# Sums of the mixing layer's end on GpSimd and VectorE, and two pairs' weight sums moved into the attention: a decoder trunk on one Trainium2 core

## The chip, the core and the metric

One core of a Trainium2 chip (trn2) runs the whole kernel in one launch. The metric is the device time of one execution in microseconds, median of several runs; the profile is of one execution, with its own time beside it. Engines are named as in the profile: PE is TensorE, DVE is VectorE, ACT is ScalarE, POOL is GpSimd, SP is the engine that issues most DMAs.

## The reference

One decoder layer on 1024 tokens of width 1024, in float32:

```python
xn = rmsnorm(x, norm_mix_w)
da_q, da_k, da_v, sw_q, sw_k, sw_v, g_da, g_sw = split_cols(xn @ w_in)
y_da = diff_attention(da_q, da_k, da_v, lam, lam_init, subln_w)      # 4 heads, causal, ALiBi
y_sw = sliding_window_attention(sw_q, sw_k, sw_v, sinks)             # 8 heads, window 128
merged = sigmoid(g_da) * (y_da @ w_br_da) + sigmoid(g_sw) * (y_sw @ w_br_sw)
x = x + merged @ w_mix_out                                           # the mixing layer's end
xn = rmsnorm(x, norm_ffn_w)
x = x + conv_ffn(xn, w_up, conv_w, conv_b, w_down)                   # up-projection to 2 x 2816, conv, SwiGLU, down
return rmsnorm(x, norm_final_w)
```

## The kernel before, in words

Everything is held transposed: 128 channels on the partitions, tokens along the free dimension. Each float32 operand is split into a high part (cast on ScalarE) and a low part (the rest, subtracted on VectorE), and a product takes three matmuls of 128x128 by 128x512: high by high, high by low, low by high.

The large products use a two-by-two block scheme with seven products (P1 to P7, as in Strassen's and Winograd's forms) in place of eight. It needs sums of blocks: of the weights (S1 to S4) and of the activations (T1 to T4).

The stages, in order: `project` (input projection; nine pairs of column blocks through the seven products), `attention` (four differential heads u = 0 to 3, then two groups of sliding-window heads; gate projections are put between the blocks of queries), `rest` (branch products and gates), `mix` (merged @ w_mix_out), `hidden` (22 pairs of up-projection columns, each with convolution and SwiGLU), `down`.

**Weight sums.** The sums of the mixing layer's weights (`sums_of`, line 93) and of the first two up-projection pairs (`sums_up`, line 105; buffers `ud0`, `ud1` in DRAM) are made by DMA: a copy issued by SP, then adding DMAs issued by GpSimd. `sums_of` has 32 steps for the mixing weights and `sums_up` 16, eight copies and eight adds, each of 256 KB. Before, both are chained (line 486) and six steps are taken in each of the nine pairs of the projection (line 489), each queued behind the pair's last loads on SP (`self.sync`) and last sum on GpSimd (`self.sum`) by `issue_after`, which only fixes the order on an engine. The later pairs' sums are made on GpSimd in `sum_pair` (lines 143 to 146).

**The mixing layer's end** (`mix`, line 891). Fourteen half-stages i = 0 to 13, two for each of P1, P2, P5, P6, P3, P7, P4. Each has 24 matmuls (line 1034) and two evictions on VectorE (line 1037) that add a PSUM bank to `xm`, which holds the residual stream x. P1, P6, P7 and P4 share one set of four PSUM banks, so P4's second half may start only when P7's second half has been evicted. A finished half-row goes through `finish` (line 932): stored to DRAM, squared on ScalarE, and the squares added up on GpSimd (line 942) for the next RMSNorm.

While the last half-stages run, the activations for the first up-projection pair are made from `xm`. A hand-written table `due` (line 970) says after which half-stage which of them is traced; `run_due` queues them behind the last weight split. For each k = 0 to 3, with column block k and token halves 0 and 1:

- `scale2`: half 1 of row k is scaled by minus the norm weight, and added to half 0, which gives T1.
- `scale4`: half 1 of row k+4 is scaled into c22, which gives B22.
- `sums4`: c22 is added to half 1 of row k (which gives T3) and to half 0 of row k (which gives T2).
- `b21`, `scale3`: half 0 of row k+4 gives B21; scaled by minus the weight it is added to half 0 of row k, which gives T4.
- `t1` to `t4`, and the B forms, through `put` and `parts` (lines 914 to 928): cast on ScalarE, low part on VectorE.

Each of these sixteen sums is, before, an adding DMA from SBUF to SBUF, issued by GpSimd (`add`, line 930), so that the cast after it waits for a DMA to land.

The first pair's weights come in four parts (`part_pair`, line 117): part 0 is A11, A12; part 1 is S1, S2; part 2 is S3, S4; part 3 is A22. Each is a load by SP into one of three `raw` tiles, a cast on ScalarE (line 126) and a low part on VectorE (line 128). Before, part 1 is traced at half-stage 12 after the due work, part 0 at 13 ahead of the due work, part 2 at 13 after it, part 3 at the end. The first pair's products in `hidden` (line 1081) run in the order P1, P5, P3, P7, P2, then sixteen column sums of the squares (line 207), then P6, P4, then P1 and P2 of the second pair, and the spread of the reciprocal norms (line 222).

In `attention`, `da_at` (line 662) clears two blocks of the transposed weights on GpSimd (line 670) before each second block of queries, and `da_av` (line 708) multiplies them with the values after it, four times in a head. `v32` (line 643) loads a head's values through SP.

Of the kernel before, what the change touches and what calls it, by code (L numbers as in the profile page):

```python
# [3 lines left out]

# [1 line left out]

# [5 lines left out]
F32 = mybir.dt.float32  # L12
F32R = mybir.dt.float32r
AF = mybir.ActivationFunctionType
ALU = mybir.AluOpType
# [31 lines left out]
class Trunk:  # L47
# [260 lines left out]
    def project(self):  # L308
# [6 lines left out]
        with ExitStack() as ctx:  # L315
# [158 lines left out]
            for m in self.plain[3:]:  # L474
# [4 lines left out]
                if m == self.plain[3]:  # L479
                    with tc.issue_after(self.pow.ins), tc.high_priority(40):  # L480
                        wg, pg = self.next_w(), [bank() for _ in range(2)]
                    for hf in range(2):
                        self.mm3(pg[hf], wg, self.xact, hf)
            prods = (("P1", "A11", "B11"), ("P2", "A12", "B21"), ("P5", "S1", "T1"), ("P7", "S3", "T3"), ("P3", "S4", "B22"),
                     ("P6", "S2", "T2"), ("P4", "A22", "T4"))
            sums = chain(self.sums_of(self.md, self.w_mix, H2), self.sums_up())
            for j, ms in enumerate(self.pairs):
                w = self.next_w()
                for _ in range(6):
                    with tc.issue_after(self.sync), tc.issue_after(self.sum):  # L490
                        next(sums, None)
                pp = {}
                for name, a, b in (prods[i] for i in ((0, 1, 4, 2, 3, 5, 6) if j == 0 else (0, 1, 2, 5, 3, 4, 6))):
                    pp[name] = bank()
                    self.product(pp[name], w[a], b)
                us = [self.tl(tp, [P, T], "us", bufs=3) for _ in range(2)]
                self.recombine(pp, us, tp, 0)
                for m, u in zip(ms, us):
                    if self.kind[m] == "g":
                        nc.sync.dma_start(self.gd[m - 18], u)  # L500
                    else:
                        nc.gpsimd.tensor_tensor(u, u, self.rstd, ALU.mult)  # L502
                        self.keep(m, u, (tp, "hi"))
# [38 lines left out]
    def attention(self):  # L542
        nc, tc = self.nc, self.tc
        with ExitStack() as ctx:
            e = ctx.enter_context
            self.ap = e(tc.tile_pool(name="ap", bufs=1, side="right", reuse_waits="tile"))
            self.fpool = e(tc.tile_pool(name="fyp", bufs=1, side="right", reuse_waits="tile"))
            ap = self.ap

            lt = self.tl(self.gpool, [P, 64], "g", bufs=2)  # L550
            ls = self.st.tile([P, 4], F32, name="ls")
            for c in range(2):
                a = C_LAM + 128 * c
                nc.vector.tensor_tensor(lt, self.vecs[:, a:a + 64], self.vecs[:, a + 64:a + 128], ALU.mult)
                nc.vector.tensor_reduce(ls[:, c:c + 1], lt, axis=mybir.AxisListType.X, op=ALU.add)
            nc.scalar.activation(ls[:, 2:4], ls[:, 0:2], AF.Exp)
            self.neglam = self.cp.tile([P, 1], F32, name="neglam")
            nc.vector.tensor_tensor(self.neglam, ls[:, 3:4], ls[:, 2:3], ALU.subtract)
            nc.vector.tensor_scalar(self.neglam, self.neglam, LAM_INIT, None, ALU.subtract)
            self.nsink = self.cp.tile([P, 8], F32, name="nsink")  # L560
            nc.vector.tensor_scalar(self.nsink, self.vecs[:, C_SINK:C_SINK + 8], -1.0, None, ALU.mult)
            self.subw = self.cp.tile([P, 1], F32, name="subw")
            nc.vector.tensor_scalar(self.subw, self.vecs[:, C_SUB:C_SUB + 1], 1.0 - LAM_INIT, None, ALU.mult)

            self.bias = ap.tile([P, T + 256], F32, name="bias")
            nc.sync.dma_start(self.bias, self.bias_d)

            later = []
            st = self.q_stacks(0), self.kv_stacks(0)
            for b in self.back[0][0]:  # L570
                self.back_half(*b)
            for u in range(6):
                if st is None:
                    st = self.q_stacks(u), self.kv_stacks(u)
                if u < 4:
                    self.v_parts(u)
                elif u == 4:
                    self.sw_v(self.v32(17))
                y = self.tl(self.fpool, [P, T], "y", bufs=2) if u < 4 else None
                aT = None  # L580
                for i in range(NB):
                    if u < 4:
                        if i == 0:
                            self.s0 = self.tl(self.st, [P, NB], "s0", bufs=2)
                        if i % 2 == 0:
                            aT = self.da_at(i // 2)
                        self.da_step(u, i, st, aT)
                        if i % 2 == 1:
                            self.da_av(u, i // 2, aT, y)
                    else:  # L590
                        self.sw_step(u - 4, i, st)
                    for b in self.back[u + 1][i]:
                        self.back_half(*b)
                    self.flush(1)
                    if later:
                        later.pop(0)()
                st = None
                if u < 4:
                    later = self.da_norm(u, y)
            self.flush(0)  # L600
# [42 lines left out]

    def v32(self, m):
        v = self.tl(self.fpool, [P, T], "f", bufs=2)
        self.nc.sync.dma_start(v, self.qd[m, 0])
        return v

    def v_parts(self, u):
# [12 lines left out]
    def da_at(self, r):  # L662

        t = {}
        for g in range((2 * r + 2 + 3) // 4):
            for part in range(2):
                t[g, part] = self.tl(self.ap, [P, 4, 256], "aT", F32R, bufs=5)
        for part in range(2):
            j = 2 * r + 1
            self.nc.gpsimd.memset(t[j // 4, part][:, j % 4, 0:P].bitcast(F32), 0.0)  # L670
        return t

    def da_step(self, h, i, st, aT):
# [217 lines left out]
    def mix(self, M, mr, mctx):  # L891
# [35 lines left out]
            t = self.slot(k) if name == "T3" else self.slot(4 + k) if name == "B21" else up[name, k]  # L927
            self.B[name, k] = parts(t, src, scale)

        add = lambda x, y: nc.gpsimd.dma_start(x, y, accum_op=ALU.add)  # L930

        def finish(m, hf):
            x, k = col(m, hf), m % 4
# [15 lines left out]
        def scale2(k):  # L949
            x = col(k, 1)  # L950
            nc.scalar.mul(x, x, nw[:, k:k + 1])
            add(col(k, 0), x)

        c22 = lambda k: x22[k // 2][:, k % 2]

# [1 line left out]
            nc.scalar.mul(c22(k), col(k + 4, 1), wcol(k + 4))  # L957
            put("B22", k, c22(k))

        def sums4(k):  # L960
            add(col(k, 1), c22(k))
            add(col(k, 0), c22(k))

        def scale3(k):
            nc.scalar.mul(col(k + 4, 1), col(k + 4, 0), nw[:, k + 4:k + 5])
# [1 line left out]

        t1, t2, t3, t4 = (lambda k, n=n, h=h: put(n, k, col(k, h)) for n, h in (("T1", 0), ("T2", 0), ("T3", 1), ("T4", 0)))
        b21 = lambda k: put("B21", k, col(k + 4, 0), nw[:, k + 4:k + 5])
        due = {6: ((scale1, 0, 1),), 7: ((scale1, 2, 3),), 10: ((scale2, 0, 1),), 11: ((t1, 0, 1), (scale2, 2, 3), (scale4, 0, 1), (sums4, 0, 1)),  # L970
               12: ((scale4, 2, 3), (t1, 2, 3), (sums4, 2, 3), (t3, 0, 1)), 13: ((t3, 2, 3), (t2, 0, 1), (b21, 0), (scale3, 0), (b21, 1), (scale3, 1)),
               14: ((b21, 2), (t2, 2), (b21, 3), (t2, 3), (scale3, 2, 3), (t4, 0, 1), (t4, 2, 3))}

        def split_m(name, o, hf, scale=None):
            for k in range(4):
# [11 lines left out]
        with tc.tile_pool(name="psM", bufs=8, space=PSUM, reuse_waits="tile") as psM:  # L987
            chains = [[self.tl(psM, [P, H2], "m") for _ in range(4)] for _ in range(2)]
            for n, stage in enumerate(STAGES):
# [8 lines left out]
                for h in range(2):  # L998
                    with tc.high_priority(60):
                        w = self.next_w()  # L1000
                    if i == 13:
                        w0.update(self.part_pair(pair, 0))
                    if n == 0:
                        for m in (2 * h, 2 * h + 1, 2 * h + 4, 2 * h + 5):
                            nc.sync.dma_start(xm[m], self.xT[m])
                    run_due(i)
                    held = lows[-1] if lows else None
                    first = self.lo
                    if stage == "P4":
                        self.uw = uw  # L1010
                        w0.update(self.part_pair(pair, 1 + h))
                        self.uw = None
                    if h == 0:
                        with tc.issue_after(self.hi.ins), tc.issue_after(self.lo.ins):
# [453 lines left out]
```

## Time and profile before

| | us |
|---|---|
| median of 3 runs | 1337.36 (1334.35 to 1337.37) |
| profiled execution | 1337.29 |
| its span, first to last instruction | 1335.5 |
| TensorE busy | 1307.9 |
| VectorE busy | 1059.9 |
| ScalarE busy | 637.6 |
| GpSimd busy | 513.5 |

Places in the span, from the timeline: the projection ends near 238 us, the differential heads run to about 405, P7's second half of `mix` begins near 652, P4's second half at 665.65, the first up-projection pair at 678.49, and the long run of the other pairs goes from 718 to 1112. The matmuls' ends are modelled, and the spans of GpSimd are rough; a wait is put down to the instruction that released it last.

### The profile page before, as it was taken

To read this page: it belongs to the slowest core of one execution; us is meant where nothing else is said; L and a number is where in the kernel's file an instruction comes from. 1 tells how busy PE (TensorE), PEld (TensorE's weight loads), DVE (VectorE), ACT (ScalarE), POOL (GpSimd) and SP (SyncE) were. 2 spreads that over 40 slices of the span, in tenths; PEclk is the share of its full clock that TensorE was granted. 3 is DMA by queue.
4 is the path that set the end of the run, shared out by engine and by line. 5 is a ranking of instruction groups with operands and counts; after the bars stand their busy time and mean duration, and the time that the engine had idled before them with its cause. 6 is when DMAs were issued, how large, how long until landed. Compare 5 with 4: busy or idle time off the path is not lost.

```text
span 1335.5 us, 17341 instructions
## 1 busy us (share of the span) xinstructions
PE 1307.9 (98%) x6162; PEld 1086.4 (81%) x6162; DVE 1059.9 (79%) x1504; ACT 637.6 (48%) x1010; POOL 513.5 (38%) x411
## 2 busy tenths in 40 slices
PE   9999999999999999999979999999999999999997
PEld 7888888788888878888757888888888888888886
DVE  8845763389888977567567999999999999896865
ACT  8523231276667764335564343434344435554543
POOL 0456664000011015743444667676666742000002
PEclk9999999999999999999989999999999999999998
DMA  8356876976544236568693534663536227953534
GB/s 299 120 158 207 258 186 182 312 193 176 153 126 127 95 123 220 153 210 246 180 234 111 188 124 125 161 225 104 184 122 181 75 87 255 322 186 116 166 97 146
DMA packets 86598, 231.67 MB, mean 173 GB/s; under 512 B 9584, under 2 KB 17392, under 8 KB 86256
## 3 DMA queue, kind: packets, MB, share of 16 engines
q1 hardware_dynamic: 63264, 187.04, 41.6%
q0 software_dynamic: 10368, 26.22, 11.7%
q10 hardware_dynamic: 12880, 17.31, 3.6%
q8 instruction: 48, 0.79, 0.2%
q14 instruction: 38, 0.31, 0.1%
HBM read 173.39 MB, written 84.41 MB: 193 GB/s over the span
## 4 chain that ended last, share of the span: by engine, by line
PE 83%; POOL 4%; DMA 4%; issue 3%; DVE 2%; ACT 2%; SPq 0%; POOLq 0%; ACTq 0%; DVEq 0%
PE t L1061 34%; PE y L1281 9%; PE d L1281 7%; PE g L199 4%; PE g L200 4%; PE g L201 4%; PE m L1034 4%; PE sc L687 3%; POOL us L502 2%; PE t L703 1%; PE sc L201 1%; PE sc L200 1%; PE sc L199 1%; PE t L806 1%; PE sc L775 1%
## 5 line engine op out<-in xcount | busy, mean ns | idle before, releaser
L180 DVE TENSOR_TENSOR wl<-raw,wh 128x1024 fp32r<-128x1024 f32 (+2 forms) x91 | 107.8, 1186 | 48.9 <-ACT wh L178 40.9
L178 ACT CAST wh<-raw 128x1024 fp32r<-128x1024 f32 (+2 forms) x91 | 80.6, 887 | 105.0 <-PE y L1281 49.0
L1211 POOL TENSOR_TENSOR us<-us,rstd 128x1024 f32<-128x1024 f32 x42 | 95.4, 2319 | 48.3 <-DVE us L520 29.1
L1061 PE MATMUL t<-T,sh 128*128 128x512 f32 x352 | 108.5, 390 | 0.0
L216 POOL TENSOR_TENSOR rs<-ms,mhalf 128x8 f32<-128x8 f32 (+2 forms) x9 | 14.2, 1578 | 236.6 <-DVE ms L214 230.4
L143 POOL TENSOR_TENSOR sf<-rv 128x512 f32<-128x512 f32 x29 | 60.0, 2070 | 105.9 <-DMA rv<-in_w_up 48.0
L1225 ACT ACTIVATE c<-us,vecs 128x1024 f32<-128x1024 f32 x44 | 54.7, 1247 | 78.3 <-POOL us L1211 73.9
L157 ACT CAST sh<-sf 128x1024 fp32r<-128x1024 f32 x58 | 60.0, 1043 | 49.3 <-POOL us L1210 24.4
L159 DVE TENSOR_TENSOR sl<-sf,sh 128x1024 fp32r<-128x1024 f32 x58 | 74.2, 1280 | 10.7 <-ACT sh L157 10.7
L1061 PE MATMUL t<-x,wh 128*128 128x512 f32 x248 | 82.2, 389 | 0.0
L1061 PEld LDWEIGHTS t<-T,sh 128*128 128x128 f32 x352 | 65.9, 188 | 13.6
L199 PE MATMUL g<-xh,wh 128*128 128x512 f32 x176 | 71.1, 404 | 3.2 <-DVE u L518 1.8
L1228 DVE SCALAR_TENSOR_TENSOR c<-us,vecs,c 128x1024 f32<-128x1024 f32 x44 | 71.2, 1651 | 0.1
L1227 DVE SCALAR_TENSOR_TENSOR c<-us,vecs,c 128x1024 f32<-128x1024 f32 x44 | 68.5, 1585 | 2.6 <-ACT c L1225 2.6
L200 PE MATMUL g<-x,wh 128*128 128x512 f32 x176 | 70.5, 400 | 0.0
L201 PE MATMUL g<-xh,wl 128*128 128x512 f32 x176 | 70.3, 399 | 0.0
L1061 PE MATMUL t<-T,sl 128*128 128x512 f32 x176 | 68.5, 389 | 0.0
L1061 PE MATMUL t<-x,sh 128*128 128x512 f32 x212 | 68.2, 389 | 0.0
L1281 PE MATMUL y<-h,wh 128*128 128x512 f32 (+1 forms) x224 | 65.3, 375 | 0.0
L145 POOL TENSOR_TENSOR sf<-raw,rv 128x512 f32<-128x512 f32 x29 | 52.2, 1801 | 30.8 <-DVE sl L159 30.8
L159 DVE TENSOR_TENSOR wl<-raw,wh 128x1024 fp32r<-128x1024 f32 x29 | 63.8, 2199 | 0.1
L1034 PE MATMUL m<-x,wh 128*128 128x512 f32 x192 | 60.3, 396 | 2.4 <-DVE xm L1037 2.4
(340 smaller groups left out, 3954.4 us busy)
## 6 DMA issues: line engine op xcount, KB each, us to landing
u<-qd SPq DMA_DIRECT2D x72, 256.0 KB, 6.4
raw<-in_w_in SPq DMA_DIRECT2D x22, 512.0 KB, 5.5
raw<-in_w_up SPq DMA_DIRECT2D x22, 512.0 KB, 5.0
hd<-c SPq DMA_DIRECT2D x22, 512.0 KB, 2.6
sdP<-in_w_down POOLq DMA_DIRECT2D x16, 704.0 KB, 8.7
rv<-in_w_up SPq DMA_DIRECT2D x20, 512.0 KB, 4.5
hc<-hd SPq DMA_DIRECT2D x33, 256.0 KB, 4.6
gr<-gd SPq DMA_DIRECT2D x16, 512.0 KB, 4.6
```

What stands on the lines that cost most here:

```text
L159: low = nc.vector.tensor_tensor(lo, src, hi.bitcast(F32), ALU.subtract)
L178: self.hi = nc.scalar.copy(wh, raw)
L180: self.lo = (eng or nc.vector).tensor_tensor(wl, raw, wh.bitcast(F32), ALU.subtract)
L199: nc.tensor.matmul(ps, wh[:, kc + o, :], ah, start=first and n == 0, stop=False)
L200: nc.tensor.matmul(ps, wh[:, kc + o, :], al, start=False, stop=False)
L201: nc.tensor.matmul(ps, wl[:, kc + o, :], ah, start=False, stop=last and n == len(kcs) - 1)
L1034: nc.tensor.matmul(ps, v[:, m % 2 * 4 + k, :], x, start=start and k == j == 0, stop=k == 3 and j == 2, skip_group_check=True)
L1061: nc.tensor.matmul(ps, (ah, ah, al)[p][:, k, :], (bh, bl, bh)[p], start=first and n == p == 0, stop=last and p == 2 and n == len(ks) - 1, ...
L1211: i = (nc.vector if m % NF == 0 else nc.gpsimd).tensor_tensor(us[:, 2:], us[:, 2:], self.rstd, ALU.mult)
L1227: nc.vector.scalar_tensor_tensor(c, us[:, 1:T + 1], cw[1], c, ALU.mult, ALU.add)
L1228: nc.vector.scalar_tensor_tensor(c, us[:, 0:T], cw[0], c, ALU.mult, ALU.add)
L1281: nc.tensor.matmul(ps, v[:, k - k0, :], x, start=start and k == i == 0, stop=k == HK - 1 and i == 2, skip_group_check=True)
```

## The change

`add` becomes a `tensor_tensor` add in place, on GpSimd by default. The four adds of `scale2` and the first two of the new `sum3` go to VectorE, the other ten (`sum3` for k = 2, 3, four of `sum2`, four of `scale3`) to GpSimd. `sums4` is taken apart into `sum3` and `sum2`, and the order within `due` changes. Part 1 of the first pair's weights stays at half-stage 12, parts 0 and 2 are both traced at 13 ahead of the due work.

`sums_up` is no longer chained into the projection, which takes four steps a pair instead of six. One step of it is taken after each `da_av` of the four differential heads, queued on SP behind the head's load of v and on GpSimd behind the last clearing of blocks.

```diff
-            sums = chain(self.sums_of(self.md, self.w_mix, H2), self.sums_up())
+            sums = self.sums_of(self.md, self.w_mix, H2)
...
-                for _ in range(6):
+                for _ in range(4):
...
-            later = []
+            later, sums = [], self.sums_up()
...
                             self.da_av(u, i // 2, aT, y)
+                            with tc.issue_after(self.sync), tc.issue_after(self.sum):
+                                next(sums, None)
...
-        self.nc.sync.dma_start(v, self.qd[m, 0])
+        self.sync = self.nc.sync.dma_start(v, self.qd[m, 0]).ins
...
-            self.nc.gpsimd.memset(t[j // 4, part][:, j % 4, 0:P].bitcast(F32), 0.0)
+            self.sum = self.nc.gpsimd.memset(t[j // 4, part][:, j % 4, 0:P].bitcast(F32), 0.0).ins
...
-        add = lambda x, y: nc.gpsimd.dma_start(x, y, accum_op=ALU.add)
+        add = lambda x, y, eng=nc.gpsimd: eng.tensor_tensor(x, x, y, ALU.add)
...
-            add(col(k, 0), x)
+            add(col(k, 0), x, nc.vector)
...
-        def sums4(k):
-            add(col(k, 1), c22(k))
-            add(col(k, 0), c22(k))
+        sum3 = lambda k: add(col(k, 1), c22(k), nc.vector if k < 2 else nc.gpsimd)
+        sum2 = lambda k: add(col(k, 0), c22(k))
...
-        due = {6: ((scale1, 0, 1),), 7: ((scale1, 2, 3),), 10: ((scale2, 0, 1),), 11: ((t1, 0, 1), (scale2, 2, 3), (scale4, 0, 1), (sums4, 0, 1)),
-               12: ((scale4, 2, 3), (t1, 2, 3), (sums4, 2, 3), (t3, 0, 1)), 13: ((t3, 2, 3), (t2, 0, 1), (b21, 0), (scale3, 0), (b21, 1), (scale3, 1)),
-               14: ((b21, 2), (t2, 2), (b21, 3), (t2, 3), (scale3, 2, 3), (t4, 0, 1), (t4, 2, 3))}
+        due = {6: ((scale1, 0, 1),), 7: ((scale1, 2, 3),), 10: ((scale2, 0, 1),), 11: ((t1, 0, 1), (scale2, 2, 3), (scale4, 0, 1), (sum3, 0, 1), (sum2, 0, 1)),
+               12: ((t1, 2, 3), (t3, 0, 1), (scale4, 2, 3), (sum3, 2, 3), (sum2, 2, 3)), 13: ((t3, 2, 3), (t2, 0, 1), (b21, 0), (scale3, 0), (b21, 1), (scale3, 1)),
+               14: ((t2, 2, 3), (b21, 2), (scale3, 2), (b21, 3), (scale3, 3), (t4, 0, 1, 2, 3))}
...
                     if i == 13:
-                        w0.update(self.part_pair(pair, 0))
+                        self.uw = uw
+                        for part in (0, 2):
+                            w0.update(self.part_pair(pair, part))
+                        self.uw = None
...
-                    if stage == "P4":
+                    if i == 12:
                         self.uw = uw
-                        w0.update(self.part_pair(pair, 1 + h))
+                        w0.update(self.part_pair(pair, 1))
                         self.uw = None
```

1 line of the change is left out of this document (removed).

## The prediction, made before the result was known

> **What bounds the kernel now.** I read the page's busy line first, then TensorE's waits for the stretch in which the change works, then the engines' timelines there.
>
> ```profile
> PE 1307.9 (98%) x6162; PEld 1086.4 (81%) x6162; DVE 1059.9 (79%) x1504; ACT 637.6 (48%) x1010; POOL 513.5 (38%) x411
> ```
>
> TensorE is busy for 98% of the span. Its matmul count does not change, so time can only come from the places where it stands still or runs at a lower clock. Its waits from 640 to 720 us:
>
> ```profile
> PE t L1061 <- ACT wh L126: 7.0, 2, 5.5
> PE m L1034 <- DVE xm L1037: 2.4, 1, 2.4
> PE t L1061 <- ACT sh L126: 1.4, 1, 1.4
> PE t L1061 <- DVE wl L128: 1.4, 1, 1.4
> PE t L1061 <- DVE sl L128: 0.8, 1, 0.8
> ```
>
> These sum to 13.0 us. Where they lie, from TensorE's timeline (start, duration; the wait before it in brackets), then the chain's row for the long stretch behind them, then the windows' row for the stretch (length; busy TensorE, weight load, VectorE, ScalarE, GpSimd; granted clock, DMA share, GB/s):
>
> ```profile
> 662.90 0.39 PE L1034 MATMUL m<-x,wl 128*128 128x512 f32 x1
> 665.65 0.78 PE L1034 MATMUL m<-x,wh 128*128 128x512 f32 x2 [2.36 <-DVE xm L1037]
> ...
> 678.49 1.22 PE L1061 MATMUL t<-B,wh 128*128 128x512 f32 x2 [5.53 <-ACT wh L126]
> ...
> 688.04 0.73 PE L1061 MATMUL t<-B,sh 128*128 128x512 f32 x2 [1.43 <-ACT sh L126]
> ...
> 699.05 1.84 PE L207 MATMUL t<-ones,rstd 128*128 128x1 f32 x16
> 700.76 0.72 PE L1061 MATMUL t<-T,sh 128*128 128x512 f32 x2
> ...
> 708.19 0.73 PE L1061 MATMUL t<-B,wh 128*128 128x512 f32 x2 [1.43 <-ACT wh L126]
> ...
> 717.07 1.03 PE L222 MATMUL t<-ident,rs 128*128 128x128 f32 x8
> ```
> ```profile
> 718.10 394.43 PE t L1061 x1740
> ```
> ```profile
> 663.29:717.07 53.78, 40.74 (x149) 30.89 (x149) 35.22 (x45) 27.41 (x44) 25.96 (x25) 0.84 0.79 206
> ```
>
> A full-speed matmul takes 394.43/1740 = 0.2267 us. From 663.29 (the end of P4's first half) to 717.07 TensorE has 24 matmuls of P4's second half, 84 of the first up-projection pair and 24 of the second: 132 x 0.2267 = 29.9 us, and 16 column sums from 699.05 to 700.76, 1.7 us. That is 31.6 of work in 53.8: **22.2 us are lost**, 13.0 standing still and 9.2 at a lower clock (0.84 granted). This is what the change can win here.
>
> What makes TensorE wait is ScalarE, in order, waiting for the adding DMAs (ScalarE's waits, 640 to 720; then two links of the chain):
>
> ```profile
> ACT T L918 <- DMA xm<-xm: 12.9, 5, 4.4
> ACT x L918 <- DMA xm<-c: 9.4, 4, 4.7
> ```
> ```profile
> 648.90 6.46 DMA xm<-xm
> ...
> 665.10 6.46 DMA xm<-c
> ```
>
> ScalarE stands 22.3 us for the sums of T1 to T4. Behind those casts are queued the weight casts (L126) that the first pair's matmuls need, and on VectorE the low parts behind which the evictions (L1037) are held.
>
> **The change, part by part.** *Removed:* sixteen adding DMAs of line 930, each 0.88 us of issue on GpSimd and 6.3 us to landing. *Added:* sixteen adds of 128x512. The nearest rows (min, median, max in ns):
>
> ```profile
> L930 POOL DMA_DIRECT2D xm<-xm x8: 862/880/1224, 648.9 to 694.8; - x8
> ...
> DMA to landing us min/median/max: 3.3/6.3/9.8
> ```
> ```profile
> L919 DVE TENSOR_TENSOR T<-xm,T x12: 678/686/1772, 656.0 to 705.3; 128x512 fp32r<-128x512 f32 x12
> ```
> ```profile
> L942 POOL TENSOR_TENSOR rstd<-rstd,sqs x10: 1265/1289/1682, 611.9 to 674.2; 128x512 f32<-128x512 f32 x10
> ```
>
> Six go to VectorE (four of scale2, two of sum3): 6 x 0.69 = 4.1 us. Ten go to GpSimd: 10 x 1.29 = 12.9 us, in place of 16 x 0.88 = 14.1 us of issue, so GpSimd's queue gets no longer. What a cast waits for a sum falls from 6.4 us to 0.7 or 1.3.
>
> *First wait (2.36).* The evictions of P7's second half are held behind B22's low parts, and these stood behind T1's casts on ScalarE:
>
> ```profile
> 655.39 0.62 ACT L918 CAST T<-xm 128x512 fp32r<-128x512 f32 x1 [2.11 <-DMA xm<-xm]
> ...
> 658.42 0.62 ACT L918 CAST T<-xm 128x512 fp32r<-128x512 f32 x1 [1.88 <-DMA xm<-xm]
> ```
>
> Those two waits, 4.0 us, go. Four of VectorE's adds, 2.7 us, come ahead of the evictions, partly in the time in which VectorE stood waiting too. So the evictions come between 1.3 and 4.0 us earlier, 2.36 are wanted, and more than half of that span is enough. I count this wait gone: P4 ends at 663.29 + 24 x 0.2267 = 668.7 instead of 672.96.
>
> *Second wait (5.53), the dearest.* It is for the cast and the low part of the first pair's part 0, which end at 678.44 and 679.70. The queues up to there, from the end of the last weight cast that is on time:
>
> ```profile
> 653.28:678.44 25.16, 17.32 (x69) 13.51 (x67) 12.68 (x17) 14.83 (x24) 11.70 (x13) 0.89 0.81 195
> 653.28:679.70 26.42, 18.53 (x71) 14.01 (x69) 13.91 (x19) 15.45 (x25) 12.12 (x14) 0.87 0.82 192
> ```
>
> ScalarE has 14.8 us of work in 25.2: without idle time it ends at 668.1. VectorE has 13.9 to the low part's end, and four of its adds, 2.7, fall in: 669.9 at best. TensorE wants the cast at 668.7 and the low part half a microsecond later. Neither queue will be without gaps, since scale4 waits for evictions and T3 for its sum. Between the 0.7 that VectorE's bound leaves and the old 5.5 I take **3 us left here**, in the middle, and 2 for the clock: the 24 matmuls after the 5.53 took from 678.49 to 686.61 (688.04 less its wait), 8.1 us for 5.4 of work, after a longer stop.
>
> The Trainium skill, in "TensorE: Matmul & The Clock Gate", Part 1, has the clock fall after an idle window of about 3.4 us. Here 2.36 us were enough, since P4's second half then took 7.3 us for 5.4. By the page a rest of 3 us might cost no clock, and the sum would be 2 us lower.
>
> *The later four waits (1.43, 0.84, 1.43, 1.39).* Part 2's weights stood behind B21's and T3's casts, the second pair's behind T4's DMAs. Part 2 now goes ahead of that work, so everything due at step 13 queues behind its cast on ScalarE and its low part on VectorE, and its load goes ahead on SP of part 3's. The load can start once step 13's own weights are split, by 663.3 if TensorE is not to wait; with some 6 us for a transfer, as in the links above, it lands when ScalarE has just cast part 0. I count 0 for it, up to 2 if the load is slow. The pair's last two products need T2 and T4 only after five others, 5 x 2.7 us, and over the whole stretch the two queues have 27.4 and 35.2 us of work where the new stretch is some 37 us. I count these waits gone.
>
> *Against it* stands VectorE beside GpSimd:
>
> ```profile
> 679.64 2.36 DVE L919 TENSOR_TENSOR x<-xm,x 128x512 fp32r<-128x512 f32 x1
> ```
> ```profile
> 679.83 3.31 POOL L942 TENSOR_TENSOR rstd<-rstd,rv 128x512 f32<-128x512 f32 x2
> ```
>
> The same VectorE form takes 0.69 alone: 1.7 us lost beside two GpSimd adds. Ten added GpSimd operations can so take between 0 and 12.9 us from VectorE. I take half, 6.4 us, VectorE being at work for 35.2 of the 53.8 us and not all of it with two SBUF inputs. It was idle for 18.6 of them, so about a third reaches TensorE: **2.4 us** with what it costs in clock.
>
> *Sums of the first two pairs moved into attention.* Eight copies (SP) and eight adding DMAs (GpSimd) leave the projection, and the mixing weights' sums go from six to four steps a pair. In the projection they hold GpSimd:
>
> ```profile
> 223.38 0.83 POOL L110 DMA_DIRECT2D ud<-in_w_up  x1 [8.39 <-DMA ud<-ud]
> ...
> 228.96 2.69 POOL L502 TENSOR_TENSOR us<-us,rstd 128x1024 f32<-128x1024 f32 x1
> ```
> ```profile
> 232.87 1.28 DVE L534 SCALAR_TENSOR_TENSOR us<-us,vecs,hi 128x1024 fp32r<-128x1024 f32 x1 [8.27 <-ACT hi L533]
> ```
> ```profile
> 239.35 0.47 PE L199 MATMUL g<-xh,wh 128*128 128x512 f32 x1 [1.78 <-DVE u L518]
> ```
>
> L502 stands behind the adds, VectorE (through ScalarE) behind L502, and TensorE waits 1.78 at attention's start. The last copies and their adds now lie a whole pair apart. I take 1.5 of the 1.78.
>
> In attention TensorE has no reserve, so what hides the sixteen steps matters:
>
> ```profile
> 242.00:410.00 168.00, 167.92 (x1034) 146.12 (x1033) 130.02 (x350) 105.18 (x252) 12.63 (x40) 1.00 0.66 179
> ```
> ```profile
> 291.72 0.20 POOL L670 MEMSET aT<- 128x128 f32 x1 [0.63 <-PE t L717]
> 298.11 0.35 POOL L670 MEMSET aT<- 128x128 f32 x2 [6.19 <-PE t L716]
> ```
>
> GpSimd is busy for 12.6 of 168 us. An add of 0.82 us lies between two memsets 6 us apart; behind it waits only the next memset, and for that the products with the transposed weights, most of a block later. A copy precedes its add by four steps, half a head. On SP each copy is one more issue ahead of the stack loads. Cost 0; without that cover each add's wait for its copy, 8.4 us above, would show eight times.
>
> **Sum.** The profiled execution took 1337.29 us (span 1335.5 and 1.8 around it); the median of the three runs is 1337.36, the same within 0.1. So 1337.29 - 22.2 - 1.5 + 3 + 2 + 2.4 = **1321.0 us**.
>
> **Rivals.** (a) *All of it goes*: both queues reach part 0 in time, 1337.29 - 22.2 - 1.8 = 1313.3, up to 1317. For it: ScalarE's 668.1. Against: VectorE's 669.9.
>
> (b) *VectorE becomes the bound*: GpSimd's adds take their full 12.9 from it and its own six 4.1, 17 of the 22.2: 1337.29 - 5.2 - 1.5 = 1330.6, from 1326 to 1333. For it: the row of 2.36. Against it, a form that reads PSUM:
>
> ```profile
> L1037 DVE TENSOR_TENSOR xm<-xm,m x28: 676/681/689, 596.8 to 687.7; 128x512 f32<-128x512 f32 x28
> ```
>
> None of the 28 evictions was ever lengthened, though GpSimd adds run among them. The Trainium skill, "SBUF — State Buffer", section "SBUF: two separate sides", has a VectorE operation with two SBUF inputs and a GpSimd operation that reads SBUF exclude each other for a whole instruction; the rows of 2.36 and 3.31 agree.
>
> (c) *Slower*: the same exclusion, but broken into separate stops. The first pair's products need low parts of B22, T3, B21, T2 and T4 in turn; if each comes late by its own blocked operation, TensorE stops five times and each stop costs 2 us of clock besides: 17 + 5 x 2 = 27 against 23.7 won, 1340.6. It decides where VectorE is blocked at nearly every one of the ten adds, twice what I take. Against it: VectorE's idle time.
>
> (d) *No change*: the casts wait for something other than the sums, such as the weights' loads (DMA share 0.79 here), and the 13 us return under other names, within 4 us of 1337.3. ScalarE's waits name xm's DMAs nine times, so little speaks for it.
>
> **Chances.** Forecast, 1317 to 1326: 0.58. (a) 0.15. (b) 0.19. (c) 0.05. (d) 0.03. The range leaves out (c), (d) and the outer parts of (a) and (b): 1315.5 to 1331. A measurement here tells about 0.3%, 4 us, from no change. Faster: 0.58 + 0.15 + 0.19 = 0.92; same 0.03; slower 0.05.
>
> **What would show it.** ScalarE's waits for xm's DMAs gone; the wait of 2.36 absent; P4 ending near 669; the first pair's first product starting between 669 and 673 after a wait of 0 to 4 us; the column sums near 688; the spread of 717.07 moved to near 702; L502 at the projection's end no longer behind ud, and the 1.78 gone. I am wrong if VectorE's two-input operations from 655 to 700 average well above 0.69 and TensorE waits for them several times, if GpSimd's adds come so late that T2 or T4 hold TensorE, or if waits appear in attention.

## The result, and the profile after

The changed kernel takes 1335.01 us (median of 12 runs, 1333.29 to 1341.32) and the kernel before, run beside it, 1335.57 (12 runs, 1332.25 to 1339.68). The ratio of the two means is 1.0001, with a 95% interval of 0.9985 to 1.0018: no difference. 1321.0 was predicted, with a range that ended at 1331. The same kernel run again, beside other runs of before, gave 0.9974 [0.9962, 0.9987], so it may be up to some 3 us faster; it is not 16.

The profiled execution of after took 1333.29 us (span 1331.1). From landmarks on TensorE's timeline the span divides like this:

| us | before | after |
|---|---|---|
| A: start to attention's first gate product | 239.3 | 235.6 |
| B: from there to the first matmul of `mix` | 353.1 | 359.1 |
| C: from there to the spread of the reciprocal norms | 124.7 | 117.5 |
| from there to `down` | 395.3 | 395.3 |

So the change wins in C what it was made for, though half of what was forecast, wins a little in A, and loses nearly as much in B, where nothing was expected.

**The mixing layer's end.** ScalarE's 22.3 us of waits for the adding DMAs are gone from its list. TensorE's waits of after from 640 to 720 us (total, times, longest), and where they lie on its timeline, down to the spread:

```profile
PE t L1064 <- DVE xm L1040: 3.5, 1, 3.5
PE t L1064 <- DVE wl L127: 3.0, 1, 3.0
PE m L1037 <- DVE xm L1040: 1.2, 1, 1.2
PE t L1064 <- DVE x L923: 0.7, 1, 0.7
```
```profile
666.80 0.70 PE L1037 MATMUL m<-x,wh 128*128 128x512 f32 x2 [1.25 <-DVE xm L1040]
...
675.97 0.70 PE L1064 MATMUL t<-B,wh 128*128 128x512 f32 x2 [3.47 <-DVE xm L1040]
679.70 0.79 PE L1064 MATMUL t<-B,wl 128*128 128x512 f32 x1 [3.03 <-DVE wl L127]
...
695.65 0.50 PE L1064 MATMUL t<-x,wh 128*128 128x512 f32 x1 [0.73 <-DVE x L923]
...
712.15 1.03 PE L221 MATMUL t<-ident,rs 128*128 128x128 f32 x8
```

Before there were six waits, five of them for weight parts and the longest for ScalarE. Now there are four, and every one names VectorE. By the prediction's own count: P4's first half ends at 666.80 - 1.25 = 665.55, the spread is at 712.15, 46.6 us with the same 31.6 of work in them. So 15.0 us are lost where 22.2 were: 8.5 standing still (1.25 + 3.47 + 3.03 + 0.73) and 6.5 at a lower clock. The 7.2 between them are the gain in C.

The crowded stretch, before and then after (length; busy TensorE, weight load, VectorE, ScalarE, GpSimd; granted clock, DMA share, GB/s):

```profile
655.00:698.00 43.00, 32.80 (x117) 24.92 (x116) 28.20 (x34) 27.66 (x45) 22.05 (x21) 0.84 0.88 211
```
```profile
655.00:698.00 43.00, 34.53 (x146) 27.16 (x144) 42.35 (x41) 29.91 (x49) 30.61 (x18) 0.91 0.45 155
```

VectorE goes from 28.20 to 42.35 of 43 us: it has almost no idle time left. Of these 14.2 us some 4.7 are more work: four of the six adds that it was given lie in this stretch (2.7 at 0.68 each; the other two come before 655), and three operations more than before (2.0). The remaining 9.5 are that its operations became longer. VectorE's groups of after in this stretch (count, busy us, mean ns), then two of the same groups of before:

```profile
L920 DVE TENSOR_TENSOR T<-xm,T 128x512 fp32r<-128x512 f32 x12 | 10.4, 908 | 0.5 <-ACT T L919 0.5
L923 DVE SCALAR_TENSOR_TENSOR x<-xm,ms,x 128x512 fp32r<-128x512 f32 x4 | 6.4, 1628 | 0.0
L920 DVE TENSOR_TENSOR x<-xm,x 128x512 fp32r<-128x512 f32 x4 | 5.3, 1355 | 0.0
L920 DVE TENSOR_TENSOR B<-c,B 128x512 fp32r<-128x512 f32 x4 | 4.7, 1217 | 0.0
L1040 DVE TENSOR_TENSOR xm<-xm,m 128x512 f32<-128x512 f32 x7 | 4.7, 675 | 1.0 <-PE m L1037 1.0
```
```profile
L919 DVE TENSOR_TENSOR x<-xm,x 128x512 fp32r<-128x512 f32 x4 | 4.4, 1106 | 5.9 <-ACT x L918 5.9
L919 DVE TENSOR_TENSOR B<-c,B 128x512 fp32r<-128x512 f32 x4 | 2.9, 766 | 0.9 <-ACT B L918 0.9
```

The low parts of 128x512, both of whose inputs lie in SBUF, average 0.9 to 1.6 us where they took 0.8 to 1.1 before; the shortest take 0.68 (0.74 for the form of L923). The evictions (L1040), with one input in PSUM, stay at 675 ns. How this becomes TensorE's wait of 3.47 is read from two timelines of after, GpSimd's and VectorE's:

```profile
667.84 3.49 POOL L943 TENSOR_TENSOR rstd<-rstd,sqs 128x512 f32<-128x512 f32 x2 [5.27 <-ACT sqs L942]
671.28 7.28 POOL L931 TENSOR_TENSOR xm<-xm,c 128x512 f32<-128x512 f32 x4
```
```profile
668.38 3.49 DVE L920 TENSOR_TENSOR x<-xm,x 128x512 fp32r<-128x512 f32 x2
671.80 3.43 DVE L920 TENSOR_TENSOR B<-c,B 128x512 fp32r<-128x512 f32 x2
675.15 0.68 DVE L1040 TENSOR_TENSOR xm<-xm,m 128x512 f32<-128x512 f32 x1
```

Four low parts take 6.9 us, step for step with GpSimd's adds at about 1.75 each, and the eviction that the first pair's first product wants (675.15) stands behind them.

**The attention.** By the column sums that close each head, the second head takes 40.5 us instead of 35.6; the other three are within 1 us of before. SP's rows of after in that head, GpSimd's, then ScalarE's and TensorE's:

```profile
295.02 0.59 SPq L647 DMA_DIRECT2D f<-qd  x1
302.40 1.78 SPq L108 DMA_DIRECT2D ud<-ud  x2
304.28 0.53 SPq L167 DMA_DIRECT2D raw<-in_w_in  x1
```
```profile
295.72 0.83 POOL L109 DMA_DIRECT2D ud<-in_w_up  x1 [0.40 <-issue]
...
297.10 0.81 POOL L109 DMA_DIRECT2D ud<-in_w_up  x1 [0.19 <-issue]
```
```profile
310.80 1.04 ACT L177 CAST wh<-raw 128x1024 fp32r<-128x1024 f32 x1 [3.50 <-DMA raw<-in_w_in]
```
```profile
313.19 0.39 PE L716 MATMUL t<-aT,v 128*128 128x256 f32 x1 [2.97 <-ACT aT L706]
```

SP stands from 295.6 to 302.4: the copies of L108 read what GpSimd's adding DMAs of 295.72 and 297.10 write, and wait for them to land. Behind them on SP's queue stands a load of gate weights (L167). It is issued at 304.28; ScalarE waits 3.50 us for it, the next transposed weights (L706) stand behind that cast on ScalarE, and TensorE waits 2.97. Before, a load of gate weights stood right behind the load of a head's values, with no copy between them:

```profile
272.85 0.53 SPq L646 DMA_DIRECT2D f<-qd  x1
273.50 0.35 SPq L168 DMA_DIRECT2D raw<-in_w_in  x1
```

SP's list of waits of after, 240 to 410 us, has it as its longest entry:

```profile
SPq L108 <- DMA ud<-in_w_up: 27.9, 4, 10.4
```

This stop of 2.97 is half of the 6.0 us that B lost. All waits of TensorE in B sum to 7.9 us in after and 1.8 before; the other 3.1 us of the difference are small ones, most of them behind the differential heads, and their causes were not traced.

### The profile page after: what moved, and what is told of

Same layout as the page of the kernel before. It is cut to its first block, busy times and chain, and to the rows that moved or that the text cites. A ratio compares the mean times of both kernels' runs of the same rounds, so it can differ in the third digit from the quotient of the medians.

```text
span 1331.1 us, 17305 instructions
## 1 busy us (share of the span) xinstructions
PE 1303.5 (98%) x6162; PEld 1083.9 (81%) x6162; DVE 1086.7 (82%) x1510; ACT 638.0 (48%) x1010; POOL 518.4 (39%) x405
## 4 chain that ended last, share of the span: by engine, by line
PE 74%; DVE 13%; issue 6%; DMA 3%; ACT 2%; POOL 1%; SPq 0%; POOLq 0%; ACTq 0%; DVEq 0%
PE t L1064 25%; PE y L1284 9%; PE d L1284 7%; PE m L1037 5%; PE g L198 4%; PE g L199 4%; PE g L200 4%; PE sc L688 3%; DVE wl L158 2%; DVE c L1230 2%; DVE c L1231 1%; PE t L704 1%; PE sc L198 1%; PE sc L200 1%; PE sc L199 1%
## 5 line engine op out<-in xcount | busy, mean ns | idle before, releaser
L158 DVE TENSOR_TENSOR sl<-sf,sh 128x1024 fp32r<-128x1024 f32 x58 | 81.7, 1408 | 11.5 <-ACT sh L156 11.5
L158 DVE TENSOR_TENSOR wl<-raw,wh 128x1024 fp32r<-128x1024 f32 x29 | 70.0, 2412 | 0.1
L671 POOL MEMSET aT<- 128x128 f32 x32 | 7.3, 247 | 149.4 <-PE t L717 39.4
```

Source lines behind the costliest of these rows:

```text
L158: low = nc.vector.tensor_tensor(lo, src, hi.bitcast(F32), ALU.subtract)
```

## The experiments

**Theory M**: in the mixing layer's end VectorE is the bound, its operations with two SBUF inputs held up by GpSimd's new adds. **Rival M**: it is ScalarE's queue, or the order of the work. **Theory S**: attention loses because copies wait in SP's queue ahead of gate loads. **Rival S**: the adding DMAs themselves, or their traffic, cost it. Each ratio is against runs of before on the same chip, whose medians lay between 1338.18 and 1339.42 us. In kernels with only the mixing half, line numbers are one or two off from those of after.

**1. The mixing half alone**, and **2. the attention half alone**: the other half's lines as before.

> The mixing layer's half of the change alone: sums on GpSimd and VectorE, part 2 of the weights early; the first two pairs' weight sums stay in the projection. Theory 1 (the two halves work against each other: the mixing layer's end wins about 7 us, the projection about 4, and attention loses about 6 to a copy that holds SP): the stretch from the mixing layer's first matmul to the spread falls from 124.7 us to 117 to 118, attention keeps its 353, and the whole is 5 to 8 us faster, ratio near 0.995. Rival (the mixing layer wins nothing that lasts, what it wins is given back in the pairs after it): the stretch falls but the one from the spread to the down-projection grows from 395.3 by as much, ratio 1.000.

> The other half alone: the first two pairs' weight sums made during the first attention, the mixing layer's sums still by adding DMAs. Theory 1: the projection ends some 3 to 4 us earlier (its wait of 1.78 gone), SP waits up to 10 us for an adding DMA at a copy from one half-made sum to the next, a gate's weights arrive late behind it, and the stretch from attention's first gate product to the mixing layer grows from 353.1 by 5 to 7 us: in all 1 to 4 us slower than before. Rival (the lost time in attention of the changed kernel is a chance of one execution): attention keeps its 353 and the whole is 2 to 4 us faster.

Measured: mixing half 1334.52 us, ratio 0.9956 [0.9938, 0.9973]; attention half 1342.91 us, 1.0027 [1.0014, 1.0040]. One half wins 6 us, the other loses some 4. In their profiles C is 117.5 with the mixing half, as in after, and B is 354.7 with the mixing half alone and 363.4 with the attention half alone. There the two rows of after are found again, in SP's and TensorE's lists of waits from 240 to 410 us:

```profile
SPq L108 <- DMA ud<-in_w_up: 28.6, 4, 10.5
```
```profile
PE t L716 <- ACT aT L706: 6.0, 1, 6.0
```

**3. After, once more.**

> The changed kernel once more, beside its halves on one chip: within 3 us of before. By theory 1 its profile repeats the stretches 235.6 (to attention), 359.1 (to the mixing layer), 117.5 (to the spread), each within 1 us, and the wait of 3.0 us in the second head; by chance as the rival these move by several us.

Measured: 1336.04 us, 0.9974 [0.9962, 0.9987]; A 235.6, B 362.4, C 117.5. C repeats to 0.1 us, B moves by 3: TensorE's stop at L716 is 4.0 us here.

**4. All sixteen sums on VectorE** (mixing half only).

```diff
-        add = lambda x, y, eng=nc.gpsimd: eng.tensor_tensor(x, x, y, ALU.add)
+        add = lambda x, y, eng=nc.vector: eng.tensor_tensor(x, x, y, ALU.add)
...
-        sum3 = lambda k: add(col(k, 1), c22(k), nc.vector if k < 2 else nc.gpsimd)
+        sum3 = lambda k: add(col(k, 1), c22(k), nc.vector)
```

> As the mixing half alone, but all sixteen adds on VectorE, none on GpSimd. Theory 2 (what is left of the loss at the hidden layer's start is VectorE and GpSimd excluding each other): VectorE's 128x512 operations with two SBUF inputs there go back to 0.7 us from 1.2 to 1.8, it has ten more of them (6.9 us) but loses none of the 10 to 13 us of lengthening, so the first product's low part comes some 3 to 5 us earlier and the stretch to the spread falls from 117.5 to 112 to 115. Rival (order and length of VectorE's queue alone, no exclusion): ten more adds make it 3 to 7 us longer, 120 to 124.

Measured: 1327.61 us, 0.9920 [0.9901, 0.9939], C 114.9. VectorE has ten adds more than in after, and less to do: the stretch's row and two of VectorE's groups.

```profile
655.00:698.00 43.00, 35.14 (x146) 27.80 (x146) 37.39 (x51) 28.82 (x47) 22.57 (x9) 0.92 0.44 150
```
```profile
L919 DVE TENSOR_TENSOR B<-c,B 128x512 fp32r<-128x512 f32 x4 | 2.6, 676 | 0.0
L919 DVE TENSOR_TENSOR x<-xm,x 128x512 fp32r<-128x512 f32 x4 | 2.6, 676 | 0.0
```

The same low parts that took 1217 and 1355 ns in after take 676. That is theory M: 51 operations in 37.39 us against 41 in 42.35. C falls by only 2.5 us, though, from 117.5 to 114.9. The medians of numbers 1 and 4 lie 7 us apart; what the rest is was not traced, and 1.9 of it is A, which the edit does not touch. What is left shows on the other side, in GpSimd's, ScalarE's and TensorE's timelines of this kernel:

```profile
664.65 12.99 POOL L942 TENSOR_TENSOR rstd<-rstd,sqs 128x512 f32<-128x512 f32 x2 [8.28 <-ACT sqs L941]
```
```profile
677.67 0.63 ACT L941 ACTIVATE rv<-xm 128x512 f32<-128x512 f32 x1 [5.89 <-POOL rstd L942]
```
```profile
684.51 1.03 PE L1063 MATMUL t<-B,sh 128*128 128x512 f32 x2 [4.00 <-ACT T L918]
```

Now GpSimd is the one held up: two adds of squares, 1.29 us each when alone, fill 12.99 us beside VectorE's queue, ScalarE waits for them and TensorE waits 4.00 for a cast behind that.

**5. No sums at all** (mixing half; `add` does nothing), the floor for any place to put them.

> The mixing half alone with all sixteen sums left out (T1 to T4 lack their addends; only the time counts): the floor of what any engine for the sums could reach with this order. Theory 2 (GpSimd and VectorE exclude each other): only the squares' adds of line 942 are left on GpSimd, the stretch to the spread falls to 107 to 111 us of the 102.5 without any loss. Rival (the order of the two queues is what holds TensorE): it stays within 2 us of the 114.9 with all sums on VectorE.

Measured: 1324.78 us, 0.9899 [0.9880, 0.9918], C 110.0, within the theory's 107 to 111. So the sums cost 7.5 us of C in after and 4.9 on VectorE alone. But even without any sum C is 7.5 us above the 102.5 of no loss (124.7 - 22.2), and 4.8 of them are TensorE's waits in the timeline, most of them for low parts of weights. VectorE's operations are lengthened here too, by GpSimd's adds of squares alone (last row, against 676 in number 4):

```profile
675.27 0.50 PE L1063 MATMUL t<-B,wl 128*128 128x512 f32 x1 [2.67 <-DVE wl L128]
...
698.12 0.73 PE L1063 MATMUL t<-B,wh 128*128 128x512 f32 x2 [0.53 <-ACT wh L126]
700.25 0.50 PE L1063 MATMUL t<-B,wl 128*128 128x512 f32 x1 [1.39 <-DVE wl L128]
```
```profile
L919 DVE TENSOR_TENSOR x<-xm,x 128x512 fp32r<-128x512 f32 x4 | 4.8, 1237 | 0.0
```

**6. Sums on VectorE with the scaling folded in**, which takes it from ScalarE (one `scalar_tensor_tensor` in place of a scaling and an add), to see whether ScalarE's queue binds.

```diff
-            nc.scalar.mul(x, x, nw[:, k:k + 1])
-            add(col(k, 0), x, nc.vector)
+            stt(col(k, 0), col(k, 1), nw[:, k:k + 1], col(k, 0), ALU.mult, ALU.add)
```

> The mixing half alone, all sums on VectorE and the scalings of scale2 and scale3 folded into them (x1*s + x0 in one VectorE operation), so eight ScalarE operations of 0.71 us go, 5.7 us, and VectorE's count stays as with all sums on it. Theory 2 with ScalarE's queue as the second bound: the stretch to the spread falls from 114.9 to 111 to 114 us, ratio to before near 0.990. Rival (VectorE alone bounds): 114.9 again.

Measured: 1332.67 us, 0.9957 [0.9940, 0.9973], C 119.2, worse than number 4 by 4.3 us:

```profile
655.00:698.00 43.00, 34.12 (x146) 26.99 (x145) 41.07 (x51) 24.40 (x40) 13.37 (x9) 0.92 0.46 156
```

ScalarE has 4.4 us less to do and TensorE gains nothing, so ScalarE's amount of work was not the bound. VectorE has 3.7 more for the same number of operations: the ten folded ones that lie in this stretch average 1.26 us, between 0.74 and 1.79 each, so here it is VectorE that waits beside GpSimd's adds of squares, as one of its groups shows. The order of the work also changed with this edit; what of the 4.3 us is lengthening and what is order was not taken apart.

```profile
L962 DVE SCALAR_TENSOR_TENSOR xm<-xm,ms,xm 128x512 f32<-128x512 f32 x4 | 5.0, 1258 | 0.0
```

**7. The attention half with its copies issued by GpSimd.**

```diff
-        copy = lambda n, src: lambda j: nc.sync.dma_start(d[j][:, n], src(j))
+        copy = lambda n, src: lambda j: nc.gpsimd.dma_start(d[j][:, n], src(j))
```

> The attention half alone, with its eight copies issued by GpSimd instead of SP. Theory 1 (a copy from a half-made sum waits on SP for the adding DMA, and the gate's weight load behind it comes late): SP's waits for ud vanish, the gate weights land early again, ScalarE's wait for them is gone, attention falls from 359 to 363 us back to 353 to 356 while the projection keeps its 235.6: 1 to 4 us faster than before. Rival (the same wait is now on GpSimd, ahead of the clearing of blocks that the transposed product needs): attention stays at 358 or more.

Measured: 1335.66 us, 0.9970 [0.9956, 0.9984], B 355.3. The same DMAs with the same bytes, in another queue: B is 8 us below number 2, SP's waits at the copies are gone, and the one wait that TensorE has left from 240 to 410 us is this one, for nothing that the profile shows; numbers 1, 4 and 5, whose attention is that of before, have it too (1.3, 1.3 and 2.2 us):

```profile
PE sc L688 <- issue: 1.9, 1, 1.9
```

**8. The copies on SP, but reading only the weights**, so that they have nothing to wait for.

```diff
-                     copy(1, lambda j: d[j][:, 0]), add(1, 0, 0), copy(3, lambda j: d[j][:, 1]), add(3, 0, 1)):
+                     copy(1, lambda j: row(j + NF, 0)), add(1, 0, 0), copy(3, lambda j: row(j + NF, 0)), add(3, 0, 1)):
```

> The attention half alone, with the four late copies still on SP ahead of the gate's load, but reading a row of the up-projection's weights instead of the half-made sum (so the first two pairs' weight sums S2 and S4 are not the right ones; only the time counts). Theory 1: with nothing to wait for, SP passes them in about 2 us and attention is back at 353 to 356. Rival (their traffic or their place in the queue costs the time, not the wait): 359 to 363 as with the sums.

Measured: 1336.76 us, 0.9986 [0.9973, 0.9998], B 358.4, between the two forecasts. TensorE's wait of 6.0 shrinks but stays:

```profile
PE t L716 <- ACT aT L706: 1.7, 1, 1.7
```

So, of the 8 us of B between numbers 2 and 7, the wait for the adding DMA makes 5, and the copies' mere place in SP's queue, ahead of the gate load, seems to make the other 3. The 3 are less sure than the 5: B with the attention of before reaches 357.7, and in after itself, where the stop was 2.97, B is only 0.7 us longer than here. Theory S holds with that addition; rival S falls with number 7.

**9. Both halves in their better forms**: numbers 4 and 7 together. **10.** The same with four buffers for the squares, against ScalarE's wait of 5.9 us for GpSimd.

```diff
-        sqs = [sqp.tile([P, 2, H2], F32, name="sqs")]
+        sqs = [sqp.tile([P, 2, H2], F32, name=f"sqs{n}") for n in range(2)]
```

> The two halves put together, each in the form that did best alone: all sixteen sums of the mixing layer's end on VectorE, and the first pairs' weight sums in the attention with their copies issued by GpSimd. If the two halves' gains stand beside each other (theory: they work in stretches 400 us apart and share no queue there), the projection ends near 235.7, attention to the mixing layer's first matmul takes about 355, that matmul to the spread about 115: against before 3.6 and 10 us less and some 2 more in attention, so 11 to 13 us faster, a ratio of 0.990 to 0.992, a little below all sums on VectorE alone (0.992). Rival: the weight sums that land in attention cost there what the projection gave, ratio 0.992 to 0.994, no better than all sums on VectorE alone.

> As the kernel beside it, and with four buffers in place of two for the squares that GpSimd adds up. Theory: with the sums on VectorE, GpSimd's adds of squares are what is held up (12.99 us for two adds of 1.29), ScalarE stands 5.9 us because both square buffers are full, and TensorE 4.0 us behind ScalarE's cast; with four buffers ScalarE's squares needn't wait, the 4.0 us go or fall below 1.5, and the stretch from the mixing layer's first matmul to the spread falls from 115 to 110 to 112 us, ratio 0.002 to 0.004 below its neighbour's. Rival: VectorE's own queue ends just as late (busy 37.4 of 43 us), so the wait comes back under VectorE's name and the stretch stays within 1 us of 115.

Measured: 1327.06 us, 0.9910 [0.9895, 0.9926], C 115.7; and 1325.58 us, 0.9902 [0.9884, 0.9919], C 114.6. Number 10 missed what it aimed at. ScalarE's wait is 5.85 us, as before, since the squares that wait go to another pool, opened on the space that the first one frees. It counts as a second run of number 9. The intervals of numbers 4, 9 and 10 overlap: how much the attention half adds to the gain is not settled by these ratios.

**11. Two of the adds of squares on VectorE** (those after P7's first half), and **12. those after its second half** in their place:

```diff
-                                finish(m + o, hf)
+                                finish(m + o, hf, nc.vector if i == 11 else nc.gpsimd)
```

> As the two-halves kernel with all sums on VectorE, and the two adds of squares after P7's first half, which GpSimd took 12.99 us for, on VectorE too (2 x 0.68 = 1.4 us there). In the kernel with four square buffers the wait of ScalarE did not change (5.85 us against 5.88): from P7's second half on, the squares go to other buffers anyway, which lie on the space that the first buffers give free, so that extra buffers at the first place could not take the wait away. Theory: GpSimd held up is what ScalarE waits for, and TensorE behind ScalarE's cast of T (4.2 and 3.2 us); with these two adds off GpSimd the 5.9 us go, TensorE's wait for the cast falls below 1.5, and the stretch from the mixing layer's first matmul to the spread falls from 115 to 110 to 113 us; ratio 0.986 to 0.989. Rival: VectorE's queue is as late as ScalarE's, the added 1.4 us and the low parts behind it hold TensorE in its place: the stretch stays at 114 to 116, ratio 0.990 to 0.992.

> The run before moved the wrong pair of adds: GpSimd's long entry (13.05 us for two) belongs to the squares after P7's second half, and it was still there. Here that pair, and only that pair, goes to VectorE (1.4 us). Theory, as before: ScalarE's wait of 5.8 us for GpSimd goes, TensorE's wait for the cast of T (3.4 us) falls below 1.5, the stretch from the mixing layer's first matmul to the spread falls from 114 or 115 to 110 to 112.5, ratio 0.986 to 0.989. Rival: VectorE is as late as ScalarE: the stretch stays at 113.5 to 116, and TensorE's wait returns under VectorE's name; ratio 0.989 to 0.992.

Measured: number 11 (with i == 10) 1325.56 us, 0.9897 [0.9877, 0.9917], C 114.1. The edit moved the other pair than the one of GpSimd's long entry, which is still there:

```profile
661.77 13.05 POOL L943 TENSOR_TENSOR rstd<-rstd,sqs 128x512 f32<-128x512 f32 x2 [13.11 <-ACT sqs L942]
```

Number 12: 1324.99 us, 0.9900 [0.9881, 0.9920], C 113.3. The long entry and ScalarE's wait for GpSimd are gone, and TensorE waits for VectorE instead, which is again without idle time:

```profile
655.00:698.00 43.00, 36.22 (x151) 28.08 (x150) 42.07 (x57) 28.03 (x45) 13.00 (x7) 0.92 0.49 170
```
```profile
671.58 1.19 PE L1064 MATMUL t<-B,wh 128*128 128x512 f32 x2 [3.85 <-DVE xm L1040]
...
682.12 0.70 PE L1064 MATMUL t<-B,sh 128*128 128x512 f32 x2 [1.71 <-DVE xm L1040]
```

C lies between the two forecasts, but the wait came back under VectorE's name, as the rival had it: VectorE's queue was as late as ScalarE's, and taking one wait away uncovered the other. VectorE's 42 us are not those of after: they hold 57 operations, in after 41. Numbers 9 to 12 beat both before and after, by about 1% of before.

All profiles together, by where the sums are (us):

| | kernels | stretch |
|---|---|---|
| A, pairs' sums in the projection | 5 | 236.5 to 239.3, mean 237.9 |
| A, in attention | 9 | 235.5 to 235.9, mean 235.6 |
| B, in the projection | 5 | 353.1 to 357.7, mean 355.1 |
| B, in attention, copies on SP | 3 | 359.1, 362.4, 363.4 |
| B, in attention, copies on GpSimd | 5 | 354.5 to 357.3, mean 355.5 |
| C, adding DMAs | 4 | 121.3 to 124.7 |
| C, ten sums on GpSimd | 3 | 117.5 each |
| C, all on VectorE, not folded (numbers 4, 9 to 12) | 5 | 113.3 to 115.7 |
| C, none | 1 | 110.0 |

## Why the prediction was wrong

The profile's argument about what bounded the kernel was right: the waits for adding DMAs held TensorE at the mixing layer's end, and the kernel without the sums gains 14.7 us there (124.7 to 110.0). Four steps of the sum were not right: what GpSimd costs VectorE (2.4), what the queues leave (3 + 2), the first wait and the attention (0 each).

*"About a third reaches TensorE: 2.4 us".* This step failed first. The prediction took half of GpSimd's 12.9 us as blocked time on VectorE and let two thirds of that fall into VectorE's idle time, counted over 53.8 us. But VectorE's idle time was not spare. From 655 to 698 it had 14.8 us, and the change put 14.2 more in: 4.7 of work, and some 9.5 of lengthening where 6.4 were assumed. No idle time was left to take anything up, and a late operation reached TensorE. The adds themselves were longer than counted: about 1.74 us each on GpSimd instead of 1.29, and 0.68 to 1.78 on VectorE instead of 0.69. Against the kernel without sums, those of after cost 7.5 us of C (number 5), where 2.4 were counted.

*"3 us left here", and 2 for the clock,* were too small as well. They were to cover what the queues leave at the hidden layer's start; with no sums at all C still loses 7.5 us (110.0 against 102.5). Left over in the stretch of after were thus 15.0 us; the prediction had 3 + 2 + 2.4 = 7.4. In the mixing layer the time came out near rival (b), its chance put at 0.19: it gave a gain of 5.2 there, and 7.2 came.

How much of the sums' 7.5 us is the lengthening alone is not shown. Number 4 takes GpSimd's sums away and wins 2.5, but it also gives VectorE ten more adds and holds GpSimd's squares up. What makes up the 7.5 us that stay without any sum is open too: VectorE's queue, its order and the squares beside it were not taken apart. Of rival M, the amount of ScalarE's work falls with number 6; the order of the work stays possible for that part.

*"I count this wait gone"* (2.36). It fell to 1.25. The bound of 1.3 to 4.0 us for how much earlier the evictions come was made from durations without blocking; one VectorE add of this stage took 1.78 us.

*"The later four waits … gone"* held: one of 0.73 us is left. So did the count of 0 for part 2's load: no wait of TensorE in C names its weights.

*"I take 1.5 of the 1.78"* held in direction. The wait is gone, and A is 2.3 us shorter in the mean of all profiles. The 3.7 between the two first profiles overstates it.

*"Cost 0"* for the sixteen steps in attention failed: B is 6 us longer in after and 6.5 in the mean of the three kernels with copies on SP. The prediction looked at the right resource, "on SP each copy is one more issue", and priced the issue, not the wait. Its argument, "a copy precedes its add by four steps", ran in one direction only: the later copies also follow an add, and a queue that runs in order passes that wait on to all behind it. Of the loads behind SP's copies it named those of the stacks and not the gate's; the gate load's row at 273.50 was there to be read in before.

Of the forecast gain of 14.8 us at the mixing layer's end 7.6 did not come, and attention lost 6.0 against a count of 0. The base was high besides: the sum started from 1337.29, and before's median beside after was 1335.57. The last section of the prediction had named the signs: VectorE's two-input operations well above 0.69, and waits in attention. Both are there.

The Trainium skill, "SBUF — State Buffer", section "SBUF: two separate sides", says that a VectorE operation with two SBUF inputs and a GpSimd operation which reads SBUF exclude each other for a whole instruction. The traces agree: in after VectorE's low parts take 1217 and 1355 ns beside GpSimd's sums, and in number 4, where they take 676, it is GpSimd's two adds of squares that take 12.99 us. The prediction cited it and then discounted it by half.

## What to carry to other kernels

Before work is moved from DMAs to VectorE and GpSimd together, count VectorE's idle time in the very stretch, and charge it every GpSimd operation beside which it runs two-input SBUF work; here keeping all sums on VectorE beat sharing them (C of 113.3 to 115.7 against 117.5). A DMA that reads what an earlier DMA wrote belongs in the queue that issues the earlier one, or in one with nothing urgent behind it: list what stands behind each moved DMA, and what it waits for. When a wait goes, compute the next engine's end too: number 12 took 5.8 us from ScalarE, and VectorE was just as late.

## What the runs showed of the hardware that I had not expected

*GpSimd can be shut out for long.* In after, GpSimd's adds and VectorE's low parts alternate at about 1.75 us a step. In numbers 4, 9, 10 and 11 two GpSimd adds, of 1.29 us each when alone, fill 12.99 to 13.05 us while VectorE's operations of 128x512 run at 0.68. What decides between the two patterns is not settled here.

*Short stops and the clock.* Windows of before behind its stop of 1.78 us and behind that of 2.36, then of after behind 1.25, behind 3.47 and, in attention, behind 2.97 (TensorE busy, granted clock third from the end):

```profile
239.35:244.85 5.50, 5.50 (x24) 4.58 (x25) 3.58 (x9) 1.15 (x2) 0.00 (x0) 1.00 0.98 375
665.65:673.00 7.35, 7.31 (x24) 5.54 (x24) 3.03 (x6) 2.04 (x4) 1.29 (x3) 0.77 0.94 210
```
```profile
666.80:672.50 5.70, 5.70 (x24) 4.40 (x24) 5.70 (x6) 5.39 (x8) 4.58 (x3) 1.00 0.37 142
675.97:684.00 8.03, 5.00 (x12) 3.67 (x13) 8.03 (x7) 7.12 (x12) 6.98 (x4) 0.57 0.61 177
313.19:318.19 5.00, 5.00 (x31) 4.54 (x32) 4.60 (x10) 3.24 (x7) 0.20 (x1) 1.00 0.88 331
```

After 1.25 and 1.78 us the granted clock stayed at 1.00; after 2.36 it was 0.77, and after 3.47, with the stop of 3.03 inside the window, 0.57. So the wait that was halved, the 2.36, gave back its clock as well. The length of a stop alone does not decide it, though: behind the 2.97 in attention the clock stayed at 1.00, and of two stops near 257 us, 2.17 in number 5 and 2.15 in number 12, the first was followed by 0.66 over 5 us and the second by 1.00.
